# Causal mask of four diagonal blocks: written into the cumulative gates on GpSimd instead of added by a product on TensorE

## The chip, the cores and the metric

The kernel runs on one core of a Trainium2 chip. The metric is device time in microseconds (us) of one execution, given as the median of several runs. In rows of the profile PE is TensorE (PEld its weight loads), DVE is VectorE, ACT is ScalarE, POOL is GpSimd, and SP is SyncE, whose queue issues every DMA here.

## What is computed

One sequence of 1024 tokens of width 1024 goes through two layers. The first mixes tokens by forgetting attention, the second by gated linear attention; each is followed by a SwiGLU layer, and all are normalised and modulated. The change lies in the forgetting attention: 16 heads of width 64, where every query block of 128 sees the keys up to its own last one.

```python
log_f = jax.nn.log_sigmoid(f_logit.astype(jnp.float32) + b_f.astype(jnp.float32))
cum = jnp.cumsum(log_f, axis=1).transpose(0, 2, 1)
for blk in range(S // Q_BLOCK):                    # 8 blocks of 128 queries
    qs, qe = blk * Q_BLOCK, (blk + 1) * Q_BLOCK
    logits = jnp.einsum('bqhd,bkhd->bhqk', q[:, qs:qe], k[:, :qe]).astype(jnp.float32) * scale
    logits = logits + cum[:, :, qs:qe, None] - cum[:, :, None, :qe]
    mask = (qs + jnp.arange(Q_BLOCK))[:, None] >= jnp.arange(qe)[None, :]
    logits = jnp.where(mask[None, None], logits, -jnp.inf)
    p = jax.nn.softmax(logits, axis=-1).astype(v.dtype)
    outs.append(jnp.einsum('bhqk,bkhd->bqhd', p, v[:, :qe]))
```

The term `cum[qs:qe]` is the same along a row of a softmax and drops out; only the keys' `cum` is needed.

## The kernel before

Matrices are split into a high and a low float32r part, and a product is done as three (`mm3`, lines 267 to 270) or, for scores, as two.

The attention goes through eight pairs of heads, `p` = 0 to 7, two heads `a` in each; below, head h = 2p + a. For a head, `attention` (L1177) visits four groups of two query blocks in the order `ORDER = (0, 3, 1, 2)` (L1165), that is the query blocks 0 1, 6 7, 2 3, 4 5. For each it runs `scores` and then the `outputs` of the group visited before it, which was left `pending`: so the probabilities of a group are transposed and multiplied with the values while the scores of the next group are made.

`scores` works on one query block after the other, in pieces of at most 512 keys. TensorE makes `Qs*K1` (L1102) and `Qs*KL` (L1103) in one PSUM tile, with the sign turned, and in the piece that holds the diagonal a third product, L1105, adds `maskb` with the identity as weights: a constant 128x128 bf16 tile with 1e30 above the diagonal. VectorE then adds `cm`, the cumulative gates of the head, spread over all 128 partitions, and takes the row's minimum (the "reduce", L1108). ScalarE takes the exponential and its sum (L1112), VectorE the reciprocal (L1113), and GpSimd scales the row (the "norm", L1114). In `outputs`, TensorE transposes the probabilities (L1134), both engines split them into high and low (L174, L175), and TensorE multiplies them with the values (L1146, L1148).

The cumulative gates are computed once (`gates_end`, L916 to L922), written to DRAM as `cum_d`, and read back by `load_cum(h)` (L934) as a [128, 1024] tile with the same row in every partition, 512 KB in SBUF. There are two such slots (`cumr`), so that the tile of head h+2 takes the slot of head h. The loads of heads 0 and 1 are called in `gates_end`, those of 2p+2 and 2p+3 after the pair p.

While a pair is worked on, `weave` (L130) mixes its steps, by costs that the steps yield, with the projections of the next pair (`qk_proj`, `v_half`; products L268 to L270). Their weights come through `load_w`: a DMA on SP (L209), a high part on ScalarE (L223) and a low part in quarters, three on GpSimd and one on VectorE (L227). Beside that `ada_steps` (L393) streams rows of a modulation matrix through the same three raw slots (L405 on SP) and adds them up on VectorE into `acc0` (L426), a quarter of a slot of its own. The order in which each engine's queue takes all this is settled by a scheduler when the kernel is built: from the dependencies, the program's order and a model of durations. Every queue runs strictly in that order.

Where query block 0 begins, `early` (L1100) holds the first reduces behind the last VectorE instruction of the stage before.

Of the kernel before, what the change touches and what calls it, by code (L numbers as in the profile page):

```python
# [53 lines left out]
def trunk(ctx, tc, x, c, ada_w, ada_b, norm1_g, norm2_g, ffn_w_in, ffn_w_out,  # L54
# [54 lines left out]
    def psl(t, n=1):  # L109
        return slice(t * P, (t + n) * P)  # L110
# [816 lines left out]
        split(parts[:, :, 0, :], parts[:, :, 1, :], ps.rearrange("p t (h d) -> p (t h) d", h=4))  # L927
        vts[g].append(v)

    cums = {}  # L930

    def load_cum(h):
        cums[h] = cumr([P, S], F32, f"cum{h}")
        nc.sync.dma_start(cums[h], cum_d[h].partition_broadcast(P))  # L934

# [144 lines left out]
    def scores(u):  # L1082

        p, a, g = u
        t = qkt[p]
        Qs, K1, KL = (t["QA"], t["KA"], t["KLA"]) if a == 0 else (t["QB"], t["KB"], t["KLB"])
        cm = cums[2 * p + a]
        if g < 2:
            both = lpr([P, (4 * g + 3) * P], F32, f"lp{p}{a}{g}")
            lps = [both[:, 0:(2 * g + 1) * P], both[:, (2 * g + 1) * P:]]  # L1090
        else:
            lps = [lpr([P, (2 * g + 1 + i) * P], F32, f"lp{p}{a}{g}{i}") for i in range(2)]
        st = sm.tile([P, 2, 4], F32, tag="st", bufs=4, name=f"st{p}{a}{g}")
        for qi in range(2):
            qb = 2 * g + qi
            qs, lp, Wd, mcur = psl(qb), lps[qi], (qb + 1) * P, 3e38
            cuts = (0, 384, 640) if Wd == 640 else (0, Wd) if Wd <= HALF else (0, HALF, Wd)
            for n_, (k0, k1) in enumerate(zip(cuts, cuts[1:])):
                ps = sr([P, k1 - k0], F32, f"s{p}{a}{qb}{k0}")
                early = u == (0, 0, 0)  # L1100
                diag = k1 == Wd
                nc.tensor.matmul(ps, Qs[:, qs], K1[:, k0:k1], start=True, stop=False)  # L1102
                nc.tensor.matmul(ps, Qs[:, qs], KL[:, k0:k1], start=False, stop=not diag)  # L1103
                if diag:
                    nc.tensor.matmul(ps[:, k1 - k0 - P:], identb, maskb, start=False, stop=True)  # L1105
                mnew = st[:, qi, n_:n_ + 1]
                with tc.issue_after(v_last) if early else ExitStack():
                    nc.vector.tensor_tensor_reduce(lp[:, k0:k1], ps, cm[:, k0:k1], 1.0, mcur,  # L1108
                                                   ALU.add, ALU.min, mnew)
                mcur = mnew  # L1110
                yield max(0.22, 0.00085 * (k1 - k0))
            nc.scalar.activation(lp, lp, AF.Exp, bias=mcur, scale=-1.0, accum_out=st[:, qi, 2:3])  # L1112
            nc.vector.reciprocal(st[:, qi, 3:4], st[:, qi, 2:3])  # L1113
            nc.gpsimd.tensor_scalar(lp, lp, st[:, qi, 3:4], 1.0, op0=ALU.mult, op1=ALU.mult)  # L1114
        return lps
# [61 lines left out]
    def attention(p):  # L1177
        for a in range(2):
            for g in ORDER:
                u = (p, a, g)  # L1180
                lps = yield from scores(u)
                if pending[0] is not None:
                    yield from finish(*pending[0])
                pending[0] = (u, lps)
        if p == 7:
            yield from finish(*pending[0])
# [2 lines left out]
        for g in gs:  # L1189
            yield from g  # L1190

    acc0 = acc_r([P, 2, HALF], F32, "acc0")[:, 0, 0:256]
    for j in (2, 3, 4, 5):
        ada0.q.append(ada_steps(0, j, acc0, wr, 4, 0))
    run(v_half(0, 0, gates_end))
# [2 lines left out]
    run(v_half(0, 1, lambda: split_after.update((e, last_of(e)) for e in "ADG")))  # L1198
    in_order(begin)
    v_last = last_of("D")  # L1200
    for p in range(7):
        parts = [qk_proj(p + 1, 0), qk_proj(p + 1, 1)]
        if p < 6:
            parts.insert(1, v_half(p // 2 + 1, p % 2))
        weave(attention(p), 23.0, chain(*parts), 31.0 if p < 6 else 20.8, LAGS)
        load_cum(2 * p + 2)
        load_cum(2 * p + 3)
    ada0.flush()


# [868 lines left out]
```

## Time and profile before

| | |
|---|---|
| median of 3 runs | 2410.09 us (2406.53 to 2410.24) |
| the profiled execution | 2405.74 us, of which 2404.0 us from its first to its last instruction (the span) |
| attention, first scores to last norm | from about 100 us to about 600 us of the span |
| TensorE, VectorE, ScalarE, GpSimd busy | 98%, 74%, 47%, 42% of the span |
| granted TensorE clock, mean | 0.992 |

The profile is of one execution. A row of the view by line gives the engine, what it does, how often, and its durations in ns as minimum, median and maximum; a row of the timeline gives the start and the duration in us, engine, line, output<-inputs and count; a row of the waits names who waited for whom, the total in us, how often, and the longest. [...]

### The profile page before, as it was taken

The numbers are of one execution on the slowest core, as the hardware profiler recorded it, in microseconds if no ns is written. First come the engines' busy times: TensorE is split into PE (matmuls) and PEld (weight loads), VectorE is DVE, ScalarE is ACT, GpSimd is POOL, SyncE is SP. The second block draws the span as 40 slices with busy tenths as digits, with TensorE's granted clock in tenths as the row PEclk, the third lists the DMA queues.
The fourth block names the chain that finished last, engine by engine and source line by source line (L and its number), as shares of the span: only waits on it lengthen the run. The fifth ranks groups of instructions, "written<-read, shape, count | busy, mean of one in ns | idle before, by whom it ended". The sixth has DMA issues, their size and how long they took to land.

```text
span 2404.0 us, 35757 instructions
## 1 busy us (share of the span) xinstructions
PE 2366.6 (98%) x12312; PEld 2012.2 (84%) x12312; DVE 1780.9 (74%) x3020; ACT 1126.1 (47%) x2161; POOL 1021.1 (42%) x914
## 2 busy tenths in 40 slices
PE   8999999999999999999999999999999999999998
PEld 6888888888888888888888898888888888888888
DVE  7677778886698788875797776666587767766787
ACT  5666556674443333345324555353343333345326
POOL 2333333333446666643263221222345756653362
PEclk8999999999999999999999999999999999999999
DMA  7422424342435544457654243334324434347664
GB/s 247 149 89 90 132 80 129 109 139 81 149 110 173 184 160 167 171 206 259 224 178 160 62 143 88 109 117 169 121 92 161 170 127 154 132 176 257 229 208 147
DMA packets 335774, 363.43 MB, mean 151 GB/s; under 512 B 24348, under 2 KB 277432, under 8 KB 335592
## 3 DMA queue, kind: packets, MB, share of 16 engines
q1 hardware_dynamic: 335592, 361.15, 45.0%
q8 instruction: 97, 1.59, 0.3%
q14 instruction: 85, 0.70, 0.1%
HBM read 268.19 MB, written 92.86 MB: 150 GB/s over the span
## 4 chain that ended last, share of the span: by engine, by line
PE 84%; DVE 7%; DMA 3%; ACT 2%; issue 2%; SPq 1%; POOL 1%; DVEq 0%; POOLq 0%; ACTq 0%
PE p_b L268 16%; PE p_b L270 16%; PE p_b L269 16%; PE t_b L1134 2%; PE o_b L1148 2%; PE qk_b L268 2%; PE qk_b L269 2%; PE qk_b L270 2%; PE vps_b L268 1%; PE vps_b L270 1%; PE vps_b L269 1%; PE s_b L1102 1%; PE s_b L1103 1%; PE gr_b L268 1%; PE gr_b L270 1%
## 5 line engine op out<-in xcount | busy, mean ns | idle before, releaser
L175 DVE TENSOR_TENSOR o_s<-xv_s,o_s 128x512 fp32r<-128x512 f32 (+1 forms) x376 | 320.8, 857 | 58.2 <-ACT o_s L174 57.5
L174 ACT CAST o_s<-xv_s 128x512 fp32r<-128x512 f32 (+1 forms) x376 | 217.2, 587 | 310.7 <-PE p_b L270 270.9
L269 PE MATMUL p_b<-B,o_s 128*128 128x512 f32 x608 | 237.8, 391 | 0.0
L270 PE MATMUL p_b<-B,o_s 128*128 128x512 f32 x608 | 237.4, 391 | 0.0
L268 PE MATMUL p_b<-B,o_s 128*128 128x512 f32 x608 | 236.5, 392 | 0.0
L1114 POOL TENSOR_SCALAR lp_s<-lp_s,st 128x128 f32<-128x128 f32 (+7 forms) x128 | 99.4, 782 | 290.5 <-DVE st L1113 280.5
L814 POOL TENSOR_TENSOR ex_s<-xv_s,xv_s 128x512 f32<-128x512 f32 (+1 forms) x64 | 89.2, 1394 | 267.9 <-DMA xv_s<-in_ffn_w_in_dram 98.1
L268 PE MATMUL p_b<-T,o_s 128*128 128x512 f32 x480 | 186.7, 389 | 0.0
L269 PE MATMUL p_b<-T,o_s 128*128 128x512 f32 x480 | 186.7, 389 | 0.0
L270 PE MATMUL p_b<-T,o_s 128*128 128x512 f32 x480 | 181.1, 389 | 0.0
L269 PEld LDWEIGHTS p_b<-B,o_s 128*128 128x128 f32 x608 | 114.9, 189 | 23.9
L270 PEld LDWEIGHTS p_b<-B,o_s 128*128 128x128 f32 x608 | 114.8, 189 | 23.9
L268 PEld LDWEIGHTS p_b<-B,o_s 128*128 128x128 f32 x608 | 114.8, 189 | 23.6
L1112 ACT ACTIVATE lp_s<-lp_s,st 128x128 f32<-128x128 f32 (+7 forms) x128 | 99.3, 776 | 67.1 <-DVE st L1108 64.1
L174 ACT CAST pt_s<-t_b 128x512 fp32r<-128x512 f32 (+1 forms) x160 | 79.8, 547 | 73.6 <-PE t_b L1134 73.0
L816 POOL TENSOR_TENSOR xv_s<-ex_s,xv_s 128x512 f32<-128x512 f32 (+1 forms) x64 | 85.2, 1331 | 67.7 <-DVE o_s L175 65.5
L1489 DVE TENSOR_TENSOR ex_s<-ex_s,p_b 128x512 f32<-128x512 f32 x140 | 93.7, 681 | 24.2 <-PE p_b L270 24.0
L227 POOL TENSOR_TENSOR w_l_s<-w__s,w_h_s 128x256 fp32r<-128x256 f32 x90 | 70.1, 808 | 93.0 <-ACT w_h_s L223 60.0
L175 DVE TENSOR_TENSOR pt_s<-t_b,pt_s 128x512 fp32r<-128x512 f32 (+1 forms) x160 | 96.2, 631 | 15.3 <-ACT pt_s L174 14.7
L269 PEld LDWEIGHTS p_b<-T,o_s 128*128 128x128 f32 x480 | 90.1, 188 | 18.8
L268 PEld LDWEIGHTS p_b<-T,o_s 128*128 128x128 f32 x480 | 90.1, 188 | 18.6
L270 PEld LDWEIGHTS p_b<-T,o_s 128*128 128x128 f32 x480 | 90.1, 188 | 18.6
(1956 smaller groups left out, 7397.0 us busy)
## 6 DMA issues: line engine op xcount, KB each, us to landing
xv_s<-in_ffn_w_in_dram SPq DMA_DIRECT2D x176, 256.0 KB, 3.1
hid_B<-x SPq DMA_DIRECT2D x70, 512.0 KB, 2.8
ad_s<-in_ada_w_dram SPq DMA_DIRECT2D x384, 64.0 KB, 2.3
hid_T<-x SPq DMA_DIRECT2D x36, 512.0 KB, 2.8
xv_s<-in_ffn_w_out_dram SPq DMA_DIRECT2D x96, 192.0 KB, 5.2
ada_s<-in_ada_w_dram SPq DMA_DIRECT2D x128, 128.0 KB, 2.8
xv_s<-in_ffn_w_out_dram SPq DMA_DIRECT2D x40, 256.0 KB, 3.0
T2o<-hid_T SPq DMA_DIRECT2D x18, 512.0 KB, 8.3
```

The costliest lines, as they stand in the source:

```text
L174: nc.scalar.copy(hi, src)
L175: nc.vector.tensor_sub(lo, src, hi.bitcast(F32))
L227: (nc.gpsimd if i < 3 else nc.vector).tensor_sub(lo[:, cs], rw[:, cs], hi[:, cs].bitcast(F32))
L268: nc.tensor.matmul(ps, ah, bh, start=start, stop=False)
L269: nc.tensor.matmul(ps, ah, bl, start=False, stop=False)
L270: nc.tensor.matmul(ps, al, bh, start=False, stop=stop)
L814: nc.gpsimd.tensor_add(s1, a21, a22)
L816: nc.gpsimd.tensor_sub(a11, s1, a11)
L1112: nc.scalar.activation(lp, lp, AF.Exp, bias=mcur, scale=-1.0, accum_out=st[:, qi, 2:3])
L1114: nc.gpsimd.tensor_scalar(lp, lp, st[:, qi, 3:4], 1.0, op0=ALU.mult, op1=ALU.mult)
L1134: nc.tensor.transpose(tp[:, i, :], lps[qi][:, psl(2 * b + jj)], ident)
L1489: nc.vector.tensor_add(d, d if src is None else dest(G, src), ps)
```

## The change

The mask of the query blocks 0, 1, 5 and 7 is no longer added by a product. GpSimd writes 1e30 above the diagonal into the cumulative gates themselves (`causal`, an `affine_select` in place on a 128x128 block), and the reduce adds them as it did before. Blocks 2, 3, 4 and 6 keep their product.

For block 7 this is done in the head's own tile as soon as it is loaded, since only query block 7 reads these keys. For block 5 it is done after the scores of the group of query blocks 6 and 7, which read these keys without a mask; of the later groups only query block 5 reads them. The keys of blocks 0 and 1 are read by later query blocks, so query blocks 0 and 1 get copies: a second tile of 384 columns, loaded by two more DMAs from `cum_d`, block 0 for query block 0, and blocks 0 and 1 for query block 1. Two such tiles, one for even and one for odd heads, lie in the slot of `acc0`.

`load_cum(h + 2)` and its three selects are now called in `attention`, right after the scores of the last group of head h. The order of the groups stays.

```diff
@@ -927,11 +927,26 @@
         split(parts[:, :, 0, :], parts[:, :, 1, :], ps.rearrange("p t (h d) -> p (t h) d", h=4))
         vts[g].append(v)
 
-    cums = {}
+    cums, heads_ = {}, {}
 
     def load_cum(h):
+
         cums[h] = cumr([P, S], F32, f"cum{h}")
         nc.sync.dma_start(cums[h], cum_d[h].partition_broadcast(P))
+        g = heads_[h] = acc_v[h % 2]
+        nc.sync.dma_start(g[:, 0:P], cum_d[h, 0:P].partition_broadcast(P))
+        nc.sync.dma_start(g[:, P:3 * P], cum_d[h, 0:2 * P].partition_broadcast(P))
+
+    def causal(t):
+
+        nc.gpsimd.affine_select(out=t, in_=t, pattern=[[-1, P]], compare_op=ALU.is_ge,
+                                fill=1e30, base=0, channel_multiplier=1)
+
+    def causal_first(h):
+
+        causal(cums[h][:, psl(7)])
+        causal(heads_[h][:, 0:P])
+        causal(heads_[h][:, 2 * P:3 * P])
 
 
 
@@ -1097,15 +1112,16 @@
             cuts = (0, 384, 640) if Wd == 640 else (0, Wd) if Wd <= HALF else (0, HALF, Wd)
             for n_, (k0, k1) in enumerate(zip(cuts, cuts[1:])):
                 ps = sr([P, k1 - k0], F32, f"s{p}{a}{qb}{k0}")
-                early = u == (0, 0, 0)
-                diag = k1 == Wd
+                early = u == (0, 0, ORDER[0])
+                diag = k1 == Wd and qb in (2, 3, 4, 6)
+                cmv = heads_[2 * p + a][:, qb * P:(2 * qb + 1) * P] if qb < 2 else cm[:, k0:k1]
                 nc.tensor.matmul(ps, Qs[:, qs], K1[:, k0:k1], start=True, stop=False)
                 nc.tensor.matmul(ps, Qs[:, qs], KL[:, k0:k1], start=False, stop=not diag)
                 if diag:
                     nc.tensor.matmul(ps[:, k1 - k0 - P:], identb, maskb, start=False, stop=True)
                 mnew = st[:, qi, n_:n_ + 1]
                 with tc.issue_after(v_last) if early else ExitStack():
-                    nc.vector.tensor_tensor_reduce(lp[:, k0:k1], ps, cm[:, k0:k1], 1.0, mcur,
+                    nc.vector.tensor_tensor_reduce(lp[:, k0:k1], ps, cmv, 1.0, mcur,
                                                    ALU.add, ALU.min, mnew)
                 mcur = mnew
                 yield max(0.22, 0.00085 * (k1 - k0))
@@ -1179,6 +1195,12 @@
             for g in ORDER:
                 u = (p, a, g)
                 lps = yield from scores(u)
+                h = 2 * p + a
+                if g == 3:
+                    causal(cums[h][:, psl(5)])
+                if g == ORDER[-1] and h < 14:
+                    load_cum(h + 2)
+                    causal_first(h + 2)
                 if pending[0] is not None:
                     yield from finish(*pending[0])
                 pending[0] = (u, lps)
@@ -1189,7 +1211,8 @@
         for g in gs:
             yield from g
 
-    acc0 = acc_r([P, 2, HALF], F32, "acc0")[:, 0, 0:256]
+    acc0 = acc_r([P, S], F32, "acc0")
+    acc0, acc_v = acc0[:, 0:256], [acc0[:, 256:640], acc0[:, 640:1024]]
     for j in (2, 3, 4, 5):
         ada0.q.append(ada_steps(0, j, acc0, wr, 4, 0))
     run(v_half(0, 0, gates_end))
@@ -1198,13 +1221,13 @@
     run(v_half(0, 1, lambda: split_after.update((e, last_of(e)) for e in "ADG")))
     in_order(begin)
     v_last = last_of("D")
+    causal_first(0)
+    causal_first(1)
     for p in range(7):
         parts = [qk_proj(p + 1, 0), qk_proj(p + 1, 1)]
         if p < 6:
             parts.insert(1, v_half(p // 2 + 1, p % 2))
         weave(attention(p), 23.0, chain(*parts), 31.0 if p < 6 else 20.8, LAGS)
-        load_cum(2 * p + 2)
-        load_cum(2 * p + 3)
     ada0.flush()
 
 
```

In the changed kernel's instruction order, as built, GpSimd has 64 selects more, SP has 32 DMAs more, and TensorE 64 products and 64 weight loads less.

## Prediction

> **What bounds the kernel now.** I read the page's busy times first, then the table by stage for the stage that the diff touches, then the rows of the line that goes (L1105) and the instructions around it, last the queues that get new work (POOL and SP).
>
> ```profile
> PE 2366.6 (98%) x12312; PEld 2012.2 (84%) x12312; DVE 1780.9 (74%) x3020; ACT 1126.1 (47%) x2161; POOL 1021.1 (42%) x914
> ```
> ```profile
> core 0: us, PE busy (x) PEld busy (x) DVE busy (x) ACT busy (x) POOL busy (x), PEclk, DMA share, GB/s
> 95.00:602.00 507.00, 499.07 (x3213) 436.41 (x3212) 385.48 (x991) 303.70 (x647) 185.97 (x252) 1.00 0.33 107
> ```
> The second fence is the attention, from the first scores to the last norm. TensorE is busy for 499.07 of 507.00 us there at full clock, 7.93 us are idle; DVE has 121.5 us to spare, POOL 321.0. The rest of the kernel is no looser (98% over the whole span). So a microsecond of TensorE's own work that goes in this stage should move the end by nearly a microsecond, and work put on POOL costs only where somebody waits for POOL.
>
> **The mask products that go.**
>
> ```profile
> L1105 PEld LDWEIGHTS <-identb x128: 95/95/99, 100.7 to 595.2; 128*128 128x128 bf16 x128
> L1105 PE MATMUL s_b<-maskb,identb x128: 229/229/233, 100.7 to 595.2; 128*128 128x128 bf16 x128
> ```
> 128 of them are 16 heads by 8 diagonal blocks. After the change the blocks 2, 3, 4 and 6 keep theirs; 64 go, with their 64 weight loads. The instruction order of the changed kernel, as built, has exactly these gone and no other product. What one costs is not its 229 ns, since products overlap; it is the delay of the starts behind it:
>
> ```profile
> 219.14 0.28 PE L1103 MATMUL s_b<-KLB,QB 128*128 128x256 f32 x1
> 219.26 0.23 PE L1105 MATMUL s_b<-maskb,identb 128*128 128x128 bf16 x1
> 219.30 0.48 PE L269 MATMUL qk_b<-h0l,w_h_s 128*128 128x512 f32 x1
> 219.62 0.40 PE L270 MATMUL qk_b<-h0h,w_l_s 128*128 128x512 f32 x1
> 219.85 0.39 PE L268 MATMUL qk_b<-h0h,w_h_s 128*128 128x512 f32 x1
> ```
> ```profile
> 128.54 0.23 PE L1105 MATMUL s_b<-maskb,identb 128*128 128x128 bf16 x1
> 128.57 0.36 PE L269 MATMUL vps_b<-wv_0l_s,h0h 128*128 128x256 f32 x1
> 128.78 0.28 PE L270 MATMUL vps_b<-wv_0h_s,h0l 128*128 128x256 f32 x1
> 128.89 0.28 PE L268 MATMUL vps_b<-wv_0h_s,h0h 128*128 128x256 f32 x1
> ```
> The mask itself holds the slot for 0.04 us (219.26 to 219.30). The 512-wide product after it then needs 0.32 us to the next start (219.30 to 219.62), where its like needs 0.23 (219.62 to 219.85): its 128x128 f32 weights could not load under so short a product. Together 0.13 us. With a 256-wide follower it is 0.03 + (0.21 - 0.11) = 0.13, a rounding step above what I use. Bounds for one mask: 0.04 us, if the follower's wait for its weights returned in another form, and 0.13. I take 0.12, near the upper end, because both followers shown, a wide and a narrow one, give it: 64 x 0.12 = 7.7 us, and 7.5 after the few that end in a wait anyway. Ends: 64 x 0.04 = 2.6 and 64 x 0.13 = 8.3.
>
> [...]
>
> **The new work on POOL.** Four selects of 128x128 a head, 64 in all. The only ones in the trace are two of the setup:
>
> ```profile
> L472 POOL TENSOR_SCALAR_AFFINE_SELECT mrows_s<-mrows_s x1: 294/294/294, 2.2 to 2.2; 128x128 f32<-128x128 f32 x1
> ```
> 64 x 0.294 = 18.8 us more on POOL in a stage where it idles for 321 us. Their length is covered; their place is what can cost. The select of block 5 stands, in the built order, between or just ahead of the norms (L1114) of the blocks 6 and 7, and waits for the reduce of block 7, for which the norm behind it waits anyway: nothing. The three others wait for the DMAs of head h+2, and the first norms of head h+1 (128 and 256 wide) are queued behind the first one or two of them. Who waits for those norms: the transposes (L1134) of the next head's first group. Two ends of heads, one usual and the tightest:
>
> ```profile
> 165.99 0.08 DVE L1108 DVE_READ_ACCUMULATOR2_ANT st<- 128x1 f32 x1
> 166.16 0.52 SPq L934 DMA_DIRECT2D cum_s<-cum_d  x1
> 169.22 1.20 POOL L1114 TENSOR_SCALAR lp_s<-lp_s,st 128x768 f32<-128x768 f32 x1 [6.52 <-DVE st L1113]
> 172.02 0.48 POOL L1114 TENSOR_SCALAR lp_s<-lp_s,st 128x256 f32<-128x256 f32 x1 [0.71 <-DVE st L1113]
> 175.58 0.49 PE L1134 MATMUL t_b<-ident,lp_s 128*128 128x128 f32 x3
> ```
> ```profile
> 360.13 0.08 DVE L1108 DVE_READ_ACCUMULATOR2_ANT st<- 128x1 f32 x1
> 360.24 0.34 SPq L934 DMA_DIRECT2D cum_s<-cum_d  x1
> 362.73 0.92 POOL L1114 TENSOR_SCALAR lp_s<-lp_s,st 128x768 f32<-128x768 f32 x1 [4.29 <-DVE st L1113]
> 364.16 1.16 POOL L1114 TENSOR_SCALAR lp_s<-lp_s,st 128x128 f32<-128x128 f32 x2 [0.51 <-DVE st L1113]
> 367.08 0.49 PE L1134 MATMUL t_b<-ident,lp_s 128*128 128x128 f32 x3
> ```
> ```profile
> DMA to landing us min/median/max: 3.5/3.7/7.0
> ```
> The load already leaves about 0.1 us after a head's last reduce, though the code calls it only at the end of the pair: so moving the call earlier gains nothing. It lands 3.7 us later: 169.9, before the norm of 768 ends at 170.4, and 363.9 in the tight case. There the two new loads leave at 360.6 and 360.9 and land about 364.3 and 364.6; the 128-wide norm ends at 364.5, then two selects to 365.1, the 256-wide norm to 365.6 instead of 365.3. The transposes start at 367.08, so 1.5 us are left. I count 0; if a load took the longest 7.0 us, this end would cost 1 to 2 us.
>
> **SP.** Two more DMAs a head, 64 and 128 KB, 0.34 us of issue each, behind the load they follow and waiting for reduces that are over. Behind them are queued the raw weights (L209) and the ada rows (L405).
>
> ```profile
> SPq L934 <- DVE oT_s L1163: 57.8, 7, 13.5
> SPq L934 <- DVE st L1108: 31.4, 6, 12.2
> ```
> ```profile
>   DMA ada_s<-in_ada_w_dram: 16.7, 13
> ```
> SP arrives early at 13 of these loads and waits 89.2 us in all, which hides the issue time. What can show is an ada row that arrives 0.7 us later where DVE waits for it already (13 times): at most 13 x 0.7 = 9 us of DVE, which has 121 to spare; on the path I take 0.5 us, between 0 and 2.
>
> **The start of the attention.** The first two heads have no earlier head to hide behind.
>
> ```profile
> 94.84 2.04 SPq L934 DMA_DIRECT2D cum_s<-cum_d  x2
> 96.20 2.33 POOL L227 TENSOR_TENSOR w_l_s<-w__s,w_h_s 128x256 fp32r<-128x256 f32 x3 [18.35 <-issue]
> 98.48 2.49 POOL L227 TENSOR_TENSOR wv_0l_s<-wv_s,wv_0h_s 128x256 fp32r<-128x256 f32 x3
> 100.93 2.13 POOL L227 TENSOR_TENSOR wv_4l_s<-wv_s,wv_4h_s 128x256 fp32r<-128x256 f32 x3
> 103.41 0.97 POOL L1114 TENSOR_SCALAR lp_s<-lp_s,st 128x128 f32<-128x128 f32 x2 [0.34 <-DVE st L1113]
> 101.29 0.39 PE L270 MATMUL qk_b<-h0h,w_l_s 128*128 128x512 f32 x1
> 107.55 0.28 PE L1134 MATMUL t_b<-ident,lp_s 128*128 128x128 f32 x1
> ```
> In the built order four selects stand ahead of the first split of weights (L227, at 96.20 today), two more behind the second. The second head's load becomes the fourth of six, leaves at about 95.9 and lands at 99.6; so the first split runs from 99.9 to 100.7, before the product that needs it (101.29). The other splits follow (0.78 us for two and for one, 2.49, 2.13) with two selects between, to 107.4; the two norms of 0.97 end at 108.4. The transposes that need them stand at 107.55, less 0.25 for two masks that are gone: a stall of 1.1 us. I take 1.0; ends 0, and 4 if the loads land 7.0 us after issue.
>
> **The sum.** -7.5 + 1.0 + 0.5 = -6.0 us. The profiled execution took 2405.74 us (span 2404.0 and 1.7 around it), so the sum gives it 2399.7. It is 4.35 below the median of the runs, 2410.09, which lie between 2406.53 and 2410.24; taken from the median, -6.0 gives 2404.1. I say 2404. What a measurement of this kernel can tell from no change is about 0.2%, 4.8 us.
>
> **The rivals.**
> A, the forecast: -4 to -8 us, most of it over 0.2%. Chance 0.60.
> B, the freed slot is given back: a mask costs its own 0.04 us and the follower waits for its weights, or for a buffer, in another form. 2.6 - 1.5 = 1 us, 2409. For it: 7.93 us of idle TensorE show that it sometimes does wait for others. Against it: those others have 24% or more of spare time. Chance 0.13.
> C, the start is worse: the loads land 7.0 us after issue, the first split waits until 103.2, and TensorE loses 4 us: -7.5 + 4 + 0.5 = -3, 2407. Chance 0.10.
> D, slower: POOL stands at the selects of head h+2 with the norms of head h+1 behind, and the transposes wait. In the tight case the new load leaves at 360.58; the 256-wide norm would end at landing + 0.29 + 0.48, so it passes 367.08 from a landing 5.7 us after issue; to eat all of -6.0 over 14 ends of heads, half of them as tight, takes some 0.9 us each, a landing of 6.6 us. At 9 us it is 3.3 each, 7 x 3.3 = 23, +17 us, 2427. For it: the 7.0 that one load took. Against: 3.7 in the median. Chance 0.12.
> E, DVE and POOL hold each other up:
>
> ```profile
> L426 DVE SCALAR_TENSOR_TENSOR acc_s<-ada_s,c,acc_s x124: 459/485/1230, 143.8 to 475.6; 128x256 f32<-128x256 f32 x124
> ```
> The accumulation, which reads two operands from SBUF, takes up to 1.23 us instead of 0.485 at times. If each of the 64 selects delayed one such step by its 0.294 us, DVE would lose at most 18.8 us of its 121; a fifth of that on the path is 4: -2, 2408. [...] Chance 0.05.
>
> **How the numbers follow.** Faster by over 0.2%: most of A, 0.54, and a little of C: 0.56. Within: a tenth of A, B, most of C, E: 0.31. Slower: D and the unforeseen, 0.13. The range takes in A from its upper bound (-8.3, and the spread of the runs below) to no gain, with B, C and E, and leaves out most of D: 2400 to 2411.5.
>
> **What would show it.** Right: the attention's stage shorter by about 6 us, with 64 masks, starts 0.23 us apart where one stood, an idle time of TensorE within a microsecond or two of 7.93, and later stages of equal length. B would show as longer intervals after L1103 or more waits for DVE. C: POOL's first split after 101, and TensorE idle between 101 and 109. D: TensorE waiting for norms by L1114 at the ends of heads, the selects waiting for DMA more than 2 us. E: L426 with a mean well above 0.485. I am wrong if the masks are gone, TensorE's work falls by 7 us, and the time does not follow.

## The result, and the profile after

| | median, us | runs | lowest to highest |
|---|---|---|---|
| kernel before, beside it | 2407.68 | 20 | 2403.97 to 2414.62 |
| changed kernel | 2413.45 | 20 | 2406.09 to 2417.43 |

The ratio is 1.0018, with a 95% interval from 1.0011 to 1.0026: slower, by about 4 us by this ratio and 5.8 by the two medians, where 2404.0, 6.0 us less than before, was forecast. Two later comparisons gave 1.0010 (1.0001 to 1.0019) and 1.0024 (1.0015 to 1.0033).

The page's busy times and the same stage of 507 us as in the prediction, set 4.5 us later because the profiled execution (2416.71 us) reached the attention that much later:

```profile
PE 2372.8 (98%) x12248; PEld 2017.2 (84%) x12248; DVE 1779.4 (74%) x3020; ACT 1124.8 (47%) x2161; POOL 1038.0 (43%) x978
```
```profile
core 0: us, PE busy (x) PEld busy (x) DVE busy (x) ACT busy (x) POOL busy (x), PEclk, DMA share, GB/s
99.50:606.50 507.00, 494.67 (x3137) 433.02 (x3136) 388.88 (x992) 302.37 (x645) 205.24 (x316) 1.00 0.36 113
```

POOL has 64 instructions more and 19 us more work, as worked out. TensorE's idle time in the stage has grown from 7.93 to 12.33 us. The rows of the masks and of the selects:

```profile
L1121 PE MATMUL s_b<-maskb,identb x64: 229/229/233, 116.2 to 596.3; 128*128 128x128 bf16 x64
L942 POOL TENSOR_SCALAR_AFFINE_SELECT cum_s<-cum_s x32: 285/294/481, 103.3 to 587.9; 128x128 f32<-128x128 f32 x32
L942 POOL TENSOR_SCALAR_AFFINE_SELECT acc_s<-acc_s x32: 288/294/682, 105.4 to 522.4; 128x128 f32<-128x128 f32 x32
```

So the change did what it says: 64 masks are left, and a select takes the 0.294 us that it took in the setup. How the time stands is read best from the first reduction of a head (L1108 before, L1124 after). These are the starts of heads 0 and 4 and the last instruction of head 15, before and after:

```profile
101.94 0.28 DVE L1108 CUSTOM_DVE_ANT_0 lp_s<-s_b,cum_s 128x128 f32<-128x128 f32 x1
229.97 0.29 DVE L1108 CUSTOM_DVE_ANT_0 lp_s<-s_b,cum_s 128x128 f32<-128x128 f32 x1
597.08 0.08 DVE L1108 DVE_READ_ACCUMULATOR2_ANT st<- 128x1 f32 x1
```
```profile
106.41 0.28 DVE L1124 CUSTOM_DVE_ANT_0 lp_s<-s_b,acc_s 128x128 f32<-128x128 f32 x1
240.64 0.29 DVE L1124 CUSTOM_DVE_ANT_0 lp_s<-s_b,acc_s 128x128 f32<-128x128 f32 x1
603.48 0.08 DVE L1124 DVE_READ_ACCUMULATOR2_ANT st<- 128x1 f32 x1
```

Heads 0 to 3 took 128.0 us (229.97 - 101.94) and take 134.2; heads 4 to 15 took 367.2 and take 362.9. The change loses 6.2 us in a quarter of the attention and wins 4.3 in the rest. Where a kernel was profiled more than once, these two lengths repeat within 1.8 and 0.4 us, which whole times don't do: what follows the last reduction, where all these kernels do the same work, took between 1804 and 1814 us in their profiles. So the experiments are read by these lengths first, and by the ratios beside them; most of them have one profile. The first reduction is a fair start: in the changed kernel it follows VectorE's work of the stage before at once, and the select of its tile had ended ahead of it (105.39 + 0.29 = 105.68, against 106.41).

| us, by first reductions | heads 0 to 3 | heads 4 to 15 | sum | TensorE at half clock |
|---|---|---|---|---|
| before, two profiles | 128.0, 128.0 | 367.2, 366.8 | 495.2, 494.8 | 0, 0 |
| changed, three profiles | 134.2, 135.1, 133.3 | 362.9, 362.6, 362.7 | 497.2, 497.7, 496.1 | 3.4, 6.8, 3.4 |
| e1 added work only | 133.1 | 370.6 | 503.6 | 13.6 |
| e2 removal only | 127.8 | 364.2 | 492.1 | 3.4 |
| f1 removal only, old order | 126.3 | 365.3 | 491.6 | 3.4 |
| e3 first pair masked | 129.2 | 363.9 | 493.0 | 3.4 |
| e10 no small tile at the start | 129.1 | 364.3 | 493.4 | 0 |
| e6 first product again | 132.3 | 365.0 | 497.3 | 0 |
| e8 start mended, two profiles | 127.3, 127.3 | 364.4, 364.7 | 491.7, 491.9 | 3.4, 3.4 |
| e4 late selects | 128.5 | 371.3 | 499.8 | 10.2 |
| r57 and f57, two blocks' removal only | 127.5, 127.2 | 369.3, 369.6 | 496.8, 496.7 | 0, 6.8 |
| e5 and e9, two blocks by the gates | 127.4, 127.3 | 368.7, 369.2 | 496.1, 496.5 | 0, 3.4 |
| f2 change, old order | 126.4 | 370.3 | 496.7 | 3.4 |

The last column is the time for which the granted clock stood at about 0.5 in the attention. At half clock the 512-wide products follow each other every 0.43 us instead of 0.23 (seen below), so 3.4 us of it cost about 1.6 us where TensorE has work all the time, an estimate from these two distances. The kernel before had none in either profile, so part of a difference to it can be the clock: by this estimate 6.3 us in e1, 4.7 in e4, 3.2 in f57 and one profile of the changed kernel, and 1.6 where there is one such stretch.

Where the six microseconds of the start go is seen in POOL's timeline of the changed kernel (start, length, instruction, and in brackets the idle time before it and what ended it), and in TensorE's:

```profile
103.28 0.45 POOL L942 TENSOR_SCALAR_AFFINE_SELECT cum_s<-cum_s 128x128 f32<-128x128 f32 x1 [20.62 <-issue]
105.39 0.29 POOL L942 TENSOR_SCALAR_AFFINE_SELECT acc_s<-acc_s 128x128 f32<-128x128 f32 x1 [1.66 <-DMA acc_s<-cum_d]
105.96 0.29 POOL L942 TENSOR_SCALAR_AFFINE_SELECT acc_s<-acc_s 128x128 f32<-128x128 f32 x1 [0.28 <-DMA acc_s<-cum_d]
107.22 0.29 POOL L942 TENSOR_SCALAR_AFFINE_SELECT cum_s<-cum_s 128x128 f32<-128x128 f32 x1 [0.97 <-DMA acc_s<-cum_d]
107.48 1.42 POOL L227 TENSOR_TENSOR w_l_s<-w__s,w_h_s 128x256 fp32r<-128x256 f32 x2
...
114.20 0.85 POOL L1130 TENSOR_SCALAR lp_s<-lp_s,st 128x128 f32<-128x128 f32 x2
...
117.35 0.29 POOL L942 TENSOR_SCALAR_AFFINE_SELECT acc_s<-acc_s 128x128 f32<-128x128 f32 x1 [2.30 <-DMA acc_s<-cum_d]
118.99 0.29 POOL L942 TENSOR_SCALAR_AFFINE_SELECT acc_s<-acc_s 128x128 f32<-128x128 f32 x1 [1.35 <-DMA acc_s<-cum_d]
```
```profile
108.27 0.50 PE L270 MATMUL qk_b<-h0h,w_l_s 128*128 128x512 f32 x1 [2.43 <-POOL w_l_s L227]
...
109.45 0.63 PE L270 MATMUL qk_b<-h0h,w_l_s 128*128 128x512 f32 x1
109.88 0.63 PE L268 MATMUL qk_b<-h0h,w_h_s 128*128 128x512 f32 x1
```

In the kernel before, the first split began 5.7 us ahead of the first reduction (96.20 against 101.94) and the first norm came 1.5 us behind it (103.41). Now the split begins 1.1 us behind it (107.48 against 106.41) and the norm 7.8 us (114.20). TensorE waits 2.43 us for the split, and then its products follow each other every 0.43 us instead of 0.23. In head 0 POOL stands twice more at selects of small tiles, for 3.65 us. SyncE waits for the late splits as well, since a raw slot is free only when it has been split. These are its longest waits for POOL's splits at the start, before and after:

```profile
SPq L209 <- POOL wv_0l_s L227: 2.0, 1, 2.0
```
```profile
SPq L209 <- POOL w_l_s L227: 6.3, 1, 6.3
```

The next weights left 3.4 us ahead of the first reduction (98.55 in the kernel before) and now leave 3.7 us behind it (110.12).

### The profile page after: what moved, and what is told of

It reads as the page before. It is cut to its first block, busy times and chain, and to the rows that moved or that the text cites. A ratio compares the mean times of both kernels' runs of the same rounds, so it can differ in the third digit from the quotient of the medians.

```text
span 2415.0 us, 35814 instructions
## 1 busy us (share of the span) xinstructions
PE 2372.8 (98%) x12248; PEld 2017.2 (84%) x12248; DVE 1779.4 (74%) x3020; ACT 1124.8 (47%) x2161; POOL 1038.0 (43%) x978
## 4 chain that ended last, share of the span: by engine, by line
PE 72%; DVE 12%; DMA 6%; ACT 4%; issue 3%; SPq 2%; POOL 1%; DVEq 0%; POOLq 0%; ACTq 0%
PE p_b L268 15%; PE p_b L270 15%; PE p_b L269 15%; PE o_b L1164 2%; PE t_b L1150 2%; SPq L405 2%; DMA ad_s<-in_ada_w_dram 2%; DVE acc_s L426 1%; DVE ad_s L426 1%; PE qk_b L268 1%; PE qk_b L270 1%; PE qk_b L269 1%; DMA ada_s<-in_ada_w_dram 1%; PE s_b L1118 1%; DMA xv_s<-in_ffn_w_out_dram 1%
## 5 line engine op out<-in xcount | busy, mean ns | idle before, releaser
L826 POOL TENSOR_TENSOR xv_s<-xv_s,xv_s 128x512 f32<-128x512 f32 x40 | 53.7, 1343 | 105.2 <-issue 69.0
## 6 DMA issues: line engine op xcount, KB each, us to landing
ada_s<-in_ada_w_dram SPq DMA_DIRECT2D x128, 128.0 KB, 2.9
```

What stands on the lines that cost most here:

```text
L826: nc.gpsimd.tensor_sub(r[A12], r[A12], r[A11])
```

## The experiments

**The changed kernel again** (a2, later a3) and **the kernel before again** (b2).

> The changed kernel as it is, once more, beside the three that follow. Theory S (start): POOL issues the selects of the first two heads ahead of the projections' splits and waits there for small loads, so TensorE loses about 4.2 us at the first products of the attention (2.6 us waiting, 1.6 us at half the granted clock); the rest of the loss is spread over POOL queueing (Q). Theory R (scatter): the extra 1.9 us of the attention in the changed profile is chance of that one execution. S and Q: the wait of the first qk_b product on POOL's w_l_s split is there again, 2 to 3 us, and the attention (first reduction to last reduction) lasts 496 to 498 us against 495.3 us in the profile of before; time 1.001 to 1.0025 of before. R: the wait is not there, the attention lasts about 489 us.

a2: ratio 1.0010 (1.0001 to 1.0019); attention 497.7 us, and TensorE waits 2.47 us for the split again. The loss is no chance of one profile: theory R falls.

> The kernel before once more, for its attention stage: 495.2 us in its first profile, without any half clock there. Theory G: the same within 0.5 us if the clock stays full, 1.7 us more for each stretch of 3.4 us at half clock, whose place varies (the waits near 294 and 357 us are its longest).

b2: attention 494.8 us, at full clock throughout, though this execution took 2413.96 us in all.

**The added work alone**, e1, and **the removal alone**, e2, which leaves the blocks 0, 1, 5 and 7 without their causal mask:

```
e1, against the changed kernel:
-                diag = k1 == Wd and qb in (2, 3, 4, 6)
+                diag = k1 == Wd
e2, against the kernel before:
-                diag = k1 == Wd
+                diag = k1 == Wd and qb in (2, 3, 4, 6)
```

> The added work alone: the selects and the small loads of the change stay, and all 128 products with the mask stay too (blocks 0, 1, 5, 7 are masked twice). If the products' removal is worth 0.12 us each (7.5 us) in the changed kernel, this one takes 7.5 us more than the changed kernel, about 2420 us, or 1.005 of before. If the removal is worth nothing where POOL sets the pace (theory Q strong), it is equal to the changed kernel within 2 us (1.001 to 1.003). With S alone (4.2 us at the start, nothing else) it is 1.0018 of before.

> The removal alone: the kernel of before without the 64 products with the mask of the blocks 0, 1, 5 and 7, and nothing in their place (those four blocks are left without their causal mask). Theory M (removal worth its slots): 64 x 0.12 = 7.5 us less than before, ratio 0.9969, the attention 488 us. Rival B (the freed slots are given back in waits for VectorE and POOL that come later): within 2 us of before, ratio over 0.999.

e1: 1.0024 (1.0015 to 1.0033), attention 503.6 us: with the additions alone it is 8.6 us longer, 5.1 of them in heads 0 to 3. The other 3.5 don't show that the selects cost something there, since 10.2 us of heads 4 to 15 ran at half clock:

```profile
300.50:307.30 6.80, 6.58 (x21) 5.22 (x22) 4.45 (x16) 3.29 (x9) 1.84 (x6) 0.50 0.51 169
368.80:372.20 3.40, 3.40 (x15) 3.12 (x14) 3.16 (x11) 1.96 (x6) 0.48 (x1) 0.50 0.82 231
```

For the same reason the 6.6 us from e1 to the changed kernel (503.6 less the mean of 497.0) are no clean price of the removal; the medians of e1 and a2 lie 3.5 us apart. e2: 0.9976 (0.9965 to 0.9987), attention 492.1 us: taken from the kernel before, the removal is worth 2.9 us there, and by the ratio 5.8. Both are under the 7.5 of theory M; rival B is partly right.

How much is TensorE's own can be added up from the starts of its products in the attention, kernel before against e2: the masks' own slots 5.32 and 2.87 us, the small lengthenings (under 0.12 us) of the other intervals 9.79 and 6.68, the intervals over that, which are waits or half clock, 12.15 and 14.68; the rest is 467.83 in both. So 2.45 + 3.11 = 5.6 us go, 0.087 us for each mask, and 2.5 us come back. Not all that comes back is waiting: behind a wait of 2.15 us that ended at 357.60, e2 ran at half clock for 3.4 us, which the kernel before never did in the attention:

```profile
359.20:362.60 3.40, 3.40 (x15) 3.11 (x14) 3.26 (x11) 1.78 (x5) 0.01 (x1) 0.51 0.77 219
```

The products of this stretch start about 1.4 us later in all than their like at full clock, 0.9 of it in the small lengthenings. An estimate with that set apart: about 6.4 us of work go, 0.10 us for each mask, 1.9 come back as waiting and 1.4 as half clock.

**Heads 0 and 1 as before**, e3:

```
 def load_cum(h):
     ...
+    if h < 2:
+        return
     g = heads_[h] = acc_v[h % 2]
...
-                diag = k1 == Wd and qb in (2, 3, 4, 6)
+                by_gate = 2 * p + a > 1
+                diag = k1 == Wd and (qb in (2, 3, 4, 6) or not by_gate)
...
-    causal_first(0)
-    causal_first(1)
```

> Heads 0 and 1 keep all their products with the mask and have no selects and no small loads; heads 2 to 15 as in the changed kernel. Theory S: the first splits no longer stand behind selects that wait for loads, so the 4.2 us at the start come back less 8 x 0.12 = 0.9 us for the products kept: 3.3 us under the changed kernel, ratio to before about 1.0004, and no wait of qk_b on POOL over 1 us at the start. If Q alone costs the time, it is 0.9 us over the changed kernel (1.002).

Ratio 1.0006 (0.9996 to 1.0016); heads 0 to 3 take 129.2 us instead of 134.2, the others 363.9. The start is where the time is lost in the attention; the whole time shows little of it, since a2 beside it had 1.0010 and the same median. The start isn't quite mended: in the built order the small selects of heads 2 and 3, whose tile is now free, move up to the first splits (101.47 and 102.00 in POOL's timeline of e3), and TensorE still waits 1.04 us there.

**The selects elsewhere**, e4 (all behind the norm of block 7, the small tile loaded a head earlier; head 0 keeps two products with the mask) and e5 (behind that norm too, but only blocks 5 and 7, and no small tile):

```
e4:
+                if g == 0:
+                    ...
+                    if h < 14:
+                        load_heads(h + 2)
                 if g == 3:
-                    causal(cums[h][:, psl(5)])
+                    with tc.issue_after(last_of("G")):
+                        causal(cums[h][:, psl(5)])
+                    if h < 15:
+                        causal_first(h + 1)
e5, beside this (nothing of the small tile, causal_first writes block 7 alone):
-                diag = k1 == Wd and qb in (2, 3, 4, 6)
+                diag = k1 == Wd and qb not in (5, 7)
```

> The change with its new work elsewhere: on POOL every select stands behind the norm of block 7 of the head before (no select ahead of the first splits, none that waits for a load), the small tile is loaded a head earlier, and head 0 keeps its products with the mask for blocks 0 and 1; 62 products go. Theory S+G (the loss is the stall at the start and the half clock that it brings, and the masks' removal is worth about 5.6 us of TensorE of which 2 to 3 come back as waits): attention 491 to 493 us against 497.2 and 497.7 of the changed kernel and 492.1 with the removal alone; no wait of qk_b over 1.3 us at the start; ratio to before 0.997 to 0.999. Theory Q (the selects hold POOL up wherever they stand, all through): attention 495 to 497, ratio 1.000 or more.

> Only blocks 5 and 7 by the gates, written into the tile that is there already, behind the norm of block 7; no small tile and no added load; 32 products go. S+G: half of the removal, attention about 493.5 us, ratio 0.998 to 0.9995, POOL's first splits where they were in the kernel before. If the removal is worth nothing once half of it is gone (the waits give it all back), 495 us and 1.000.

Both expectations of S+G failed; e4 is over what theory Q gave too, and e5, with 496.1 us, came nearest to its second value, 495. The start is mended in both (heads 0 to 3 take 128.5 and 127.4 us), but the other twelve heads take 371.3 and 368.7, more than before. Ratios 1.0016 (1.0005 to 1.0026) and 0.9999 (0.9990 to 1.0008). In e4 10.2 us of these heads ran at half clock; in e5 none. In e4 the ada rows come later; these rows, of b2 and of e4, are VectorE's waits for them in the attention (sum in us, times, longest):

```profile
DVE acc_s L426 <- DMA ada_s<-in_ada_w_dram: 16.0, 13, 2.7
```
```profile
DVE acc_s L426 <- DMA ada_s<-in_ada_w_dram: 24.0, 13, 4.9
```

e4 loads the small tile a head earlier, ahead of ada rows in SP's queue. That this makes a part of its loss was not tried by itself.

**The first product eleven times**, e6, so that TensorE works while it would wait:

```
     def mm3(ps, ah, al, bh, bl, start, stop, again=0):
+        for _ in range(again):
+            nc.tensor.matmul(ps, ah, bh, start=True, stop=True)
...
+            again = 10 if (p, i, hf) == (1, 0, 0) else 0
```

> The changed kernel, but the first product of the first qk_b tile is issued eleven times instead of once (each overwrites the one before), so TensorE works for 10 x 0.23 = 2.3 us where it stood idle for 2.6 us, and ends no later. Theory G (the half clock after the stall comes from the idle time): granted clock 1.00 in the 4 us after the stall, products 0.23 us apart instead of 0.43 us, attention 1.7 us shorter than 497.4 us. If the half clock has another cause, the clock is 0.5 there again and the attention 497 to 498 us.

The clock stays at 1.00 and the products 0.23 us apart, as theory G has it. Heads 0 to 3 take 132.3 us, 1 to 3 less than in the changed kernel, but no less than that, since the transposes now wait for POOL's norms (below). The other heads took 365.0 instead of 362.7 in this one profile, so the attention still takes 497.3 us, not the 1.7 less that theory G gave.

```profile
101.56 2.51 PE L269 MATMUL qk_b<-h0h,w_h_s 128*128 128x512 f32 x10
...
111.22 0.33 PE L1153 MATMUL t_b<-ident,lp_s 128*128 128x128 f32 x1 [1.35 <-POOL lp_s L1133]
```

The third profile of the changed kernel shows the stall without half clock, with no edit: TensorE waits 2.52 us there and the clock stays at 1.00 (the first row below; the second is the same stretch of the first profile, with 0.52 in the clock's column), yet heads 0 to 3 take 133.3 us against 134.2. At the start half clock was seen in three of the four profiles with a wait of over 2.4 us (e1 and two of the changed kernel) and in none of the others, so here it came with the stall, though not each time. By heads 0 to 3 of the changed kernel (134.2 and 135.1 us with it, 133.3 without) it makes 1 to 2 us of the loss; the rest is POOL's lateness.

```profile
105.00:108.40 3.40, 3.40 (x16) 2.81 (x15) 0.67 (x4) 0.60 (x2) 3.40 (x7) 1.00 0.28 68
```
```profile
109.00:112.40 3.40, 3.40 (x10) 2.63 (x9) 0.67 (x4) 0.60 (x2) 3.40 (x7) 0.52 0.28 69
```

**No small tile for heads 0 and 1**, e10; the selects of their block 7 still stand ahead of the first splits:

```
         if h < 2:
             return
         g = heads_[h] = acc_v[h % 2]
...
         causal(cums[h][:, psl(7)])
+        if h < 2:
+            return
         causal(heads_[h][:, 0:P])
```

> The changed kernel, but heads 0 and 1 have no small tile and no small loads and keep the products with the mask for blocks 0 and 1; the selects of their block 7 still stand on POOL ahead of the first splits and wait for the big loads. If the small loads are what makes the start late (they put the second head's load behind themselves and land last), the first splits come about 1 us after the first reduction, qk_b waits under 0.5 us and the attention is 492.5 to 494 us. If any select ahead of the splits is enough, qk_b waits 1.5 us or more, as much as POOL's first splits are late, and the attention is 495 us or more.

Ratio 1.0001 (0.9990 to 1.0013); heads 0 to 3 take 129.1 us, attention 493.4. TensorE waits 1.01 us, between the two expectations; the attention is as the first had it. Of the 6 to 7 us that the start costs, about 5 belong to the small tiles: their loads, and their selects that stand waiting on POOL.

**The start mended, everything else as changed**, e8 (load_heads issues the two small loads that load_cum issued, at the start behind both large ones; head 0 keeps two products with the mask):

```
+                if g == 0 and h == 0:
+                    with tc.issue_after(last_of("G")):
+                        causal(cums[0][:, psl(7)])
+                    load_heads(1)
...
+                if g == ORDER[-1] and h == 0:
+                    with tc.issue_after(last_of("G")):
+                        causal_first(1)
                 if g == ORDER[-1] and h < 14:
                     load_cum(h + 2)
-                    causal_first(h + 2)
+                    load_heads(h + 2)
+                    with tc.issue_after(last_of("G")) if h < 2 else ExitStack():
+                        causal_first(h + 2)
...
-    causal_first(0)
-    causal_first(1)
```

> The changed kernel with its places for the selects in heads 2 to 15 (block 5 ahead of the norms of blocks 6 and 7, the others at the end of the head two before), but nothing on POOL ahead of the first splits: the selects of heads 0 and 1, and the small ones of heads 2 and 3, stand behind norms of head 0; head 0 keeps its products with the mask for blocks 0 and 1; 62 products go. Theory P (the place is what costs: at the start 5 us, in e4 the place behind the norm of block 7): POOL's first norm 1.5 us after the first reduction as before (7.8 us in the changed kernel), attention 492 to 493.5 us, ratio 0.998 to 0.9995. Theory W (64 selects on POOL cost some 5 us wherever they stand): attention 496 to 498 us, ratio over 1.000.

Ratio 0.9993 (0.9982 to 1.0004), attention 491.7 us, under the 492 to 493.5 of theory P; theory W falls. POOL's first split leads again, and the norm follows the first reduction (104.39 in the profile of its second run) by 1.5 us:

```profile
98.64 2.33 POOL L227 TENSOR_TENSOR w_l_s<-w__s,w_h_s 128x256 fp32r<-128x256 f32 x3 [18.36 <-issue]
...
105.86 0.97 POOL L1133 TENSOR_SCALAR lp_s<-lp_s,st 128x128 f32<-128x128 f32 x2 [0.34 <-DVE st L1132]
106.78 0.29 POOL L944 TENSOR_SCALAR_AFFINE_SELECT cum_s<-cum_s 128x128 f32<-128x128 f32 x1
```

Once more, with the changed kernel beside it on the same chip:

> The change with the start mended, once more. If the place of the first selects is what turned the change around: attention within 1 us of 491.7 us, the first four heads about 127 us (134 in the changed kernel, 128 before), and a time 3 to 6 us under the changed kernel beside it; ratio to before 0.998 to 1.0000. If the 491.7 us were chance of one execution: 495 us or more, and a ratio over 1.0005.

> The changed kernel beside it. If the start is the cause: first four heads 134 us again, the other twelve 363 us as in the two profiles before (367 in the kernel before), attention 497 to 498 us, ratio to before 1.001 to 1.002. If chance: another division between the two.

e8: 2407.32 us, ratio 0.9988 (0.9978 to 0.9997), attention 491.9; the changed kernel 2413.21 us, 1.0024 (1.0015 to 1.0033), attention 496.1, a little under the 497 to 498 expected, and a ratio a little over. The place of the first few selects and loads is what separates faster from slower: e8 beats the changed kernel by 6 us, and the kernel before by 3 us of attention, which its two whole times put at 0.07 and 0.12%, the first within the noise.

**Two blocks only**, with selects at the changed kernel's places (e9), and with nothing in place of the products (r57, which leaves the blocks 5 and 7 without their causal mask):

```
e9, against e5:
                 if g == 3:
-                    with tc.issue_after(last_of("G")):
-                        causal(cums[h][:, psl(5)])
-                    if h < 15:
-                        causal_first(h + 1)
+                    causal(cums[h][:, psl(5)])
...
                     load_cum(h + 2)
+                    causal(cums[h + 2][:, psl(7)])
r57, against the kernel before:
-                diag = k1 == Wd
+                diag = k1 == Wd and qb not in (5, 7)
```

> As e5 (blocks 5 and 7 by the gates, no small tile, no added load), but its selects stand where the changed kernel has them: block 5 ahead of the norms of blocks 6 and 7, block 7 at the end of the head two before. Theory P: attention 493.5 us instead of the 496.1 us of e5. Theory W: 496 us again.

> The kernel of before without the 32 products with the mask of blocks 5 and 7, nothing in their place (those two blocks are left without their causal mask). If all 64 are worth the same, half of the removal's 2.9 us: attention 493.6 us against 495.0. If only the products of the blocks 0 and 1 are worth something, 495 us; if only these, 492.1 us. The distance to e9 and e5 is the price of 32 selects in either place.

e9 came out at the value of theory W, but r57 shows that the selects are not the reason, and none of its own expectations had this: r57, which only leaves out 32 products, takes 496.8 us, 1.8 more than before (ratio 1.0012, 1.0002 to 1.0022). e5 is r57 with 32 selects on POOL and the same order on every other engine, and takes 496.1; e9 takes 496.5 (1.0008, 0.9999 to 1.0017). So these 32 selects cost nothing between the norms, in either place, and the loss comes with the removal. It is not the clock, which was full in r57. By the same division of TensorE's intervals as above, about 3 us of work go in r57 and 4.6 us of waits come. TensorE waits more for VectorE's reductions, which hold the buffers of the scores, and for POOL's norms (heads 4 to 15; before, then r57):

```profile
PEld s_b L1102 <- DVE st L1108: 4.7, 8, 1.4
PEld t_b L1134 <- POOL lp_s L1114: 1.9, 2, 1.7
```
```profile
PEld s_b L1102 <- DVE st L1108: 6.4, 12, 1.2
PEld t_b L1134 <- POOL lp_s L1114: 4.2, 4, 1.9
```

**The old order kept.** The program's scheduler puts some 250 places of TensorE's order differently once products are gone. f1 and f57 repeat e2 and r57 with the order of the kernel before written down. f2 does so for the change: what both kernels have stands in the old order, selects and small loads are put between, none of them ahead of the first splits, those of the next pair at a pair's end, and head 0 keeps two products:

```
+    def order_of_before(n):
+        ...
+            for i in (seq[k] for k in at):
+                if i is not None:
+                    if last is not None:
+                        tc.add_manual_dep(i, last.name, ..., reason="order")
+                    last = i
```

> The removal alone, as in e2 (blocks 0, 1, 5 and 7 are left without their causal mask), but every engine's instructions in the attention stand in the order of the kernel before, less the 64 products. Theory O (the scheduler's new order gives the time back): 64 x 0.09 to 0.12 us come off, attention 487.5 to 489.5 us against 495.0 before and 492.1 in e2, ratio 0.9965 to 0.998. Theory B (others are late, whatever the order): 492 us again, ratio 0.9985 or so.

> As r57 (blocks 5 and 7 are left without their causal mask), the 32 products taken away with the order of before kept on every engine. Theory O: 32 x 0.09 to 0.12 us off, attention 491 to 492.2 us. Theory B: 496.8 us as in r57.

> The whole change (62 products go, head 0 keeps two) with the order of before kept for all that both kernels have; the selects and the small loads are put between: none ahead of the first splits. Theory O with P: attention within 1 us of f1, 488 to 490.5 us, ratio to before 0.997 to 0.999. If selects between the norms cost by themselves, 492 us or more.

f1 takes 491.6 us (e2: 492.1), f57 496.7 (r57: 496.8): theory O falls, the lengths come back in either order. Ratios 1.0001 (0.9993 to 1.0010) and 0.9996 (0.9987 to 1.0005): f1's whole time doesn't show the 3.4 us that its profile's attention is shorter, and f57's not the 1.7 that its is longer, which is not explained. The same removal gave 0.9976 as e2 and 1.0001 as f1, with attentions 0.5 us apart: whole times hold something beside the attention that these runs don't explain.

f2 takes 496.7 us (1.0008, 0.9998 to 1.0018), 5 more than f1, all in heads 4 to 15. That misses theory O and meets the other expectation, that selects between the norms cost by themselves; in e8, at other places, they did not. As in e4 the ada rows come later: VectorE's waits for them in heads 4 to 15 are 18.6 us in f2 and 18.4 in e4, against 12.8 in f1, 12.5 in e8 and 13.4 in the changed kernel. TensorE's weight loads wait 8.3 us for VectorE's reductions in f2 and 4.1 in f1. Whether the added loads or the selects make this was not tried.

## Why the prediction was wrong

The step that failed is **the start of the attention**: forecast 1.0 us, with an end of 4, and measured at 5.5 to 7.3 us (heads 0 to 3 of the changed kernel less the 127.8 of the removal alone). The prediction saw the right queue and the right selects ahead of the first split. It was wrong in their time: it let the second head's load leave 6.0 us ahead of the first reduction and land after 3.7 us. SP shows when the loads left:

```profile
99.66 0.35 SPq L935 DMA_DIRECT2D cum_s<-cum_d  x1
100.06 0.75 SPq L937 DMA_DIRECT2D acc_s<-cum_d  x1
100.86 0.42 SPq L938 DMA_DIRECT2D acc_s<-cum_d  x1
101.33 0.43 SPq L935 DMA_DIRECT2D cum_s<-cum_d  x1
```

The second head's load leaves 5.1 us ahead of the first reduction (101.33 against 106.41), and its select starts 5.9 us later, at 107.22; the first small load, sent at 100.06, is waited for until 105.39, 5.3 us. The 3.7 us was the median of such loads in the trace of before, where two left together at the start; here six leave, from 99.66 to 102.28 us. And the prediction counted only the first products that wait for the split: the later splits, the next weights, which wait for a split slot (6.3 us), the first norms behind them and the selects of head 2's small tile in head 0 (117.35 and 118.99) carried the delay on. e3, e10 and e8 show the cause: with heads 0 and 1 as before (e3), or without their small tile (e10), heads 0 to 3 take 129.2 and 129.1 us, and with no select ahead of the first splits (e8) 127.3. **Rival C** was this mechanism, at 4 us and with a chance of 0.10; **rival D**, POOL standing at selects with norms behind it, is the part seen in head 0, not at the ends of all heads.

**The removal**: forecast 7.5 us, measured 2.9 in the attention. The term was too large by itself, 5.6 by the starts of the products, or about 6.4 (0.10 us for a mask instead of 0.12) with the half clock set apart: what stands behind the masks alone loses 4.4 us, all small lengthenings together 3.1, and the half clock accounts for 0.9 of the difference. About 1.9 us came back as waiting, which is **rival B**; it had been given 0.13 because the other engines have spare time on the average. The 1.4 us at half clock were in no term. What the prediction says of the weights behind a mask is seen in the weight loads of the kernel before:

```profile
219.26 0.10 PEld L1105 LDWEIGHTS <-identb 128*128 128x128 bf16 x1
219.26 0.20 PEld L269 LDWEIGHTS qk_b<-h0l,w_h_s 128*128 128x128 f32 x1
219.38 0.19 PEld L270 LDWEIGHTS qk_b<-h0h,w_l_s 128*128 128x128 f32 x1
219.62 0.19 PEld L268 LDWEIGHTS qk_b<-h0h,w_h_s 128*128 128x128 f32 x1
```

The load for the product behind the mask starts with the mask, at 219.26, and takes 0.20 us, where the mask holds its slot for 0.04; for the second product after that one the load (219.62, 0.19 us) is over at 219.81, before the product starts at 219.85.

**POOL's selects in the steady state**, forecast 0: right at the places of the changed kernel, whose heads 4 to 15 take 362.7 us, with the removal alone 364.2. It is no rule: f2, with the selects and loads elsewhere, takes 5.0 us more there than f1. **SP**, forecast 0.5, lies within that. **Rival E**: L426 has a median of 0.485 us as before and a mean of 0.542 against 0.522, 2.4 us of VectorE in 124 steps; the time shows nothing of it. In the kernel before the 36 of these steps that ran beside a POOL instruction took 0.621 us in the mean and up to 1.230, the other 88 at most 0.489; in the changed kernel seven ran beside selects, and took 0.470 to 0.601.

So the sum is -2.9 for the removal, +6.4 in heads 0 to 3 and -1.5 in the others: +2.0 us, where -6.0 stood. The whole time says +2.4 to +5.8 by the three ratios. What is beyond the attention's 2 us was not located; kernels with the same work there differ by as much.

**Open** is why leaving out 32 products costs 1.8 us where leaving out all 64 wins 2.9, why f2 loses what f1 wins, and why the changed kernel gains 1.5 us on the removal alone in heads 4 to 15. What the runs show is that these heads took from 362.6 to 371.3 us, with waits for VectorE and POOL changing places and up to 10.2 us at half clock. There TensorE's work alone doesn't set the end, though it is busy 98% of the time.

## What to carry to other kernels

Before moving work onto an idle engine, write down what is queued behind it in the first microseconds, when there is no earlier work to hide a load: a few selects that waited for small loads cost more here (6.4 us) than 64 products gained (2.9). Put such work behind the first instructions that others wait for; here that turned 0.24% more into 0.12% less, measured side by side. And a product taken from an engine that is 98% busy was worth less here than its slot (2.9 us of 5.6 for 64 of them), since waits for other engines came back: measure the removal by itself, since its price can even change sign (32 of them cost 1.8 us).

## What the runs showed of the hardware

After the wait of 2.43 us TensorE ran at half clock for 3.4 us (0.52 in the row above), and in another execution of the same kernel, after 2.52 us, it did not. It happened elsewhere in the attention too: after the wait of 2.15 us in e2, and in a2 from 366.0 us on, behind a wait of 1.15 us, the longest for 14 us; a wait of 1.57 us at the like place of the kernel before, which ended at 358.49, had none behind it. No run shows what decides whether it comes. Heads 0 to 3 of the changed kernel took 134.2 and 135.1 us with such a stretch at their start and 133.3 without.

No split passed a waiting select on POOL: in the changed kernel POOL idled for 1.66, 0.28 and 0.97 us at the selects ahead of the first split, which began 1.1 us behind the first reduction; in e8, with no select ahead of it, it began 5.8 us before it (98.64 against 104.39). In the kernel before, all 3020 instructions of VectorE and all 1394 DMA issues of SyncE stand in the trace, line by line, in the order in which the program was built.
